# Diagonal tap blocks of a depthwise convolution, written ahead of time and read back as weight panels

## The chip, the cores and the metric

The kernel runs on one core of one Trainium2 chip. The metric is device time in microseconds (us) from start to end of one execution. Several engines run their own instruction streams beside each other: TensorE (PE, matmuls; PEld is its weight load), VectorE (DVE), ScalarE (ACT), GpSimd (POOL) and SyncE (SP), whose queue issues most DMAs. They meet only at semaphores.

## The reference

The program is a four-layer encoder over 512 tokens with 1024 features: retention, convolution, gated linear attention, retention, each followed by a squared-ReLU MLP. The two parts that the change touches:

```python
def rotary(t, positions):              # q and k of every retention head
    inv_freq = ROPE_BASE ** (-jnp.arange(half, dtype=F32) / half)
    ang = positions.astype(F32)[:, None, :, None] * inv_freq
    cos, sin = jnp.cos(ang), jnp.sin(ang)
    return jnp.concatenate([t1 * cos - t2 * sin, t2 * cos + t1 * sin], axis=-1)

def conformer_conv(u, w_in, b_in, w_dw, b_dw, ln_gain, ln_bias, w_out, b_out):
    a, gate = jnp.split(u @ w_in + b_in, 2, axis=-1)
    h = a * jax.nn.sigmoid(gate)
    h = lax.conv_general_dilated(h, w_dw[:, None, :], (1,), [(15, 15)],
        feature_group_count=D_MODEL) + b_dw      # 31 taps, each feature by itself
    h = jax.nn.silu(layernorm(h, ln_gain, ln_bias))
    return h @ w_out + b_out
```

The layer norm runs over the 1024 features of a token, so it needs the finished convolution of all features.

## The kernel before

Features lie on the 128 partitions and tokens along the free axis, so a tensor is eight tiles of 128x512. Every fp32 product is made of three matmuls of split operands (`mm3`, L433 to L442: high by high, low by high, high by low; the profile's L439, L440, L441). A weight panel is 128x1024: SyncE's queue loads it (512 KB), ScalarE rounds the high part, `whi` (L146), and VectorE subtracts it to get the low part, `wlo` (L147). A ring of six such pairs feeds TensorE; `Stream` (L100 to L235) fills it ahead of use. Some panels are split once, stored to DRAM in two parts and later loaded ready (`cut`).

TensorE's instructions run in the order of the code. The code also names work that is put off: `after(us, fn)` runs `fn` in the program when the matmuls written since then add up to that many us, and `flush` runs what is left. The order on ScalarE, VectorE and GpSimd is chosen by a scheduler when the program is built, except for the engines named in a `manual_schedule` block, where the code's order stands.

**The first retention** (L779 to L985). Its angles are positions times frequencies in turns, and they need more than fp32's digits: `angles` (L728 to L777) splits them into a high and a low part (`ahi`, `alo`), and GpSimd makes 24 operations of 128x512 for five larger pieces of the frequency (L757 to L764), summed up in `acc`. VectorE takes off whole turns (`wrap`, L747 to L749), adds the smaller pieces (L770) and makes a sine and a cosine (`sr`, `cr`), which also go to DRAM for the last retention. For each head, `rotated` multiplies the projected q and k by them (L850 to L852) and splits them into `qkh` and `qkl`. For head 0, TensorE does the values, q and k, then four gate projections (scaled by VectorE at L868, `o`), then the scores of q and k (`scores`, L915), which need `qkh` and `qkl`.

**The convolution** (L988 to L1187). Two projections make each feature tile (`hc`). The 31 taps of a tile are shared among the engines by the table `taps` in `run` (L1530): a pair says how many taps TensorE has, and how many ScalarE and GpSimd have together; VectorE has the rest.

- On TensorE a tap is a diagonal 128x128 matrix of that tap's weights, times the shifted tokens. ScalarE makes the high block `dh` (L1047), GpSimd the low blocks `dl`, four at a time, by an `affine_select` (L1043), while the convolution runs.
- On the side, ScalarE multiplies (L1056) and GpSimd adds (L1058, `side_taps`).
- On VectorE a tap is a multiply-add onto the sum in PSUM (L1073, `vec_taps`).

Then `center` takes a mean off and adds each tile to sums over all tiles (L1088, L252, L254). The statistics are matmuls with ones (L260); from them come the mean and the variance (L1140), and each tile is centered, scaled, put through SiLU and split into `zh` and `zl` (L1147 to L1154), the input of the output projection. All of this is done by halves of 256 tokens.

Of the kernel before, what the change touches and what calls it, by code (L numbers as in the profile page):

```python
# [21 lines left out]
P = 128  # L22
T = 512
# [71 lines left out]
class Stream:  # L95


    def __init__(self, K, src, ahead):
        self.K, self.src, self.ahead = K, src, ahead
        self.n = src.shape[0]  # L100
        self.ready, self.loaded, self.at = [], 0, 0
        self.deep = 5
        self.aside = {}
        self.cut = {}
        self.pairs, self.steps = {}, []

# [4 lines left out]
    def prep(self, parts=1):  # L111
# [8 lines left out]
        i = self.loaded  # L120
        if i in self.pairs:
            self.pair(i)
            return []
        self.loaded += 1
        if i in self.cut:
            hi, lo = self.aside.pop(i, self.ring)()
            pan = Panel(hi, lo)
            self.ready.append(pan)
            for tiles, src in zip((hi, lo), self.cut[i]):
                for t, x in enumerate(tiles):  # L130
                    nc.sync.dma_start(x.bitcast(F32), src[:, t * pan.w:(t + 1) * pan.w])
            return []
# [195 lines left out]
class Kern:  # L328
# [658 lines left out]

    def conv(self, layer, close):  # L988
        nc = self.nc
        with self.tc.tile_pool(name="conv", bufs=1) as op:  # L990
            self.W.keep(3 * KD - 4, [_spare(op, "w", 8)] * 4)
            with self.tc.tile_pool(name="taps", bufs=1) as cp:
                hc, sg = {}, {}
                co = [None] * KD
                msum = Sums(self, D)
                ident = cp.tile([P, P], F32, name="ident")
                nc.gpsimd.memset(ident, 1.0)
                nc.gpsimd.affine_select(ident, ident, pattern=[[-1, P]], compare_op=ALU.is_equal, fill=0.0, base=0, channel_multiplier=1)
# [17 lines left out]
                whi = cp.tile([P, KD * CW], F32R, name="wdh")  # L1016
                wlo = cp.tile([P, KD * CW], F32, name="wdl")
                wall = self.cst[:, _COLS["conv_w_dw"]:_COLS["conv_w_dw"] + KD * CW]
                nc.vector.tensor_copy(whi, wall)
                nc.vector.tensor_tensor(wlo, wall, whi.bitcast(F32), ALU.subtract)  # L1020
                shift = cp.tile([P, T], F32, name="shift")
                vsum = Sums(self, D)

                parts, sums = {}, {}

# [8 lines left out]
                def diag_taps(i):  # L1034

                    npe, _ = self.taps[i]
                    xh, xl = parts[i]
                    sums[i] = self.ps()
                    for t0 in range(0, npe, 4):
                        n = min(4, npe - t0)  # L1040
                        j = i * CW + t0
# [18 lines left out]
                def vec_taps(tiles, pieces=FULL):  # L1060

                    for t in range(CW):
                        for i in tiles:
# [5 lines left out]
                            if npe == 0 and t == nsw:  # L1069
# [4 lines left out]
                    for i in tiles:  # L1074
                        for lo, hi in pieces:
                            a, b = co[i][:, lo:hi], shift[:, lo:hi]
                            nc.vector.scalar_tensor_tensor(a, sums[i][:, lo:hi], self.col("conv_b_dw", i), a if self.taps[i][1] else b, ALU.add, ALU.add if self.taps[i][1] else ALU.subtract)

                def center(tiles, c=(0, T)):
                    for i in tiles:  # L1080
                        a = co[i][:, c[0]:c[1]]

                        if i == 0:
                            st = self.st()
                            nc.tensor.matmul(st, lhsT=self.ones[D], rhs=a, start=True, stop=True)
                            nc.scalar.activation(shift, st, AF.Copy, scale=float(KD))
                        if self.taps[i][1]:
                            nc.vector.tensor_tensor(a, a, shift[:, c[0]:c[1]], ALU.subtract)  # L1088
                        vsum.add(a, c)
                        msum.add(a, c, square=False)  # L1090
# [5 lines left out]

                self.lead(4, inp, us=4.0)
                pair(2)
                pair(3)
                side_taps(0)  # L1100
                side_taps(1)
                cut_taps(2)
                vec_taps((0, 1))
                self.after(self.shift_at, lambda: center((0, 1)))
# [583 lines left out]
```

## Time and profile before

| | us |
|---|---|
| median of 3 runs | 2718.35 (2717.16 to 2718.38) |
| the profiled execution's own time | 2716.43 |
| its span, first to last instruction | 2714.7 |
| TensorE busy | 2655.4 (98%) |
| VectorE busy | 1937.0 (71%) |
| ScalarE busy | 1363.1 (50%) |
| GpSimd busy | 135.2 (5%) |

The profile is of one execution. Busy times of the engines overlap each other. A wait of TensorE is given with the instruction that ended it. PEclk is the granted TensorE clock as a share of full speed.

### The profile page before, as it was taken

How to read it: one execution, taken by the hardware profiler on the slowest of the kernel's cores; microseconds unless marked ns; L12 is line 12 of the kernel's file. 1: busy time of each engine (PE TensorE's matmuls, PEld its weight loads, DVE VectorE, ACT ScalarE, POOL GpSimd, SP SyncE). 2: the span in 40 equal slices, each digit the busy share in tenths (PEclk: the TensorE clock that was granted, in tenths of full speed). 3: DMA queues.
4: the chain of work that ended last, by engine and by line, in shares of the span. 5: the costliest groups of instructions: out<-in, count | busy, mean ns of one | idle time of the engine just before them, and what ended most of it. 6: DMA issues, size and time to landing. Idle time of an engine off the chain costs nothing.

```text
span 2714.7 us, 38029 instructions
## 1 busy us (share of the span) xinstructions
PE 2655.4 (98%) x15040; PEld 2332.1 (86%) x15040; DVE 1937.0 (71%) x3045; ACT 1363.1 (50%) x2153; POOL 135.2 (5%) x133
## 2 busy tenths in 40 slices
PE   9999999999999699999999999999999999999998
PEld 7788889889998498999987888899888888989997
DVE  7755568878859977766788686777765565777766
ACT  5442445655537555544476555455544443555432
POOL 4000000000009500000000000000000000000000
PEclk9999999999999899999999999999999999999999
DMA  5223232686644012332222232333213222223322
GB/s 176 79 72 101 70 101 78 246 277 231 222 187 158 16 47 86 109 117 71 86 71 78 74 112 64 109 109 114 89 63 93 86 70 86 86 86 109 117 63 70
DMA packets 82692, 290.28 MB, mean 107 GB/s; under 512 B 9168, under 2 KB 11472, under 8 KB 82512
## 3 DMA queue, kind: packets, MB, share of 16 engines
q1 hardware_dynamic: 82368, 287.77, 32.5%
q8 instruction: 118, 1.93, 0.3%
q14 instruction: 62, 0.51, 0.1%
q10 hardware_dynamic: 144, 0.07, 0.0%
HBM read 260.02 MB, written 27.79 MB: 106 GB/s over the span
## 4 chain that ended last, share of the span: by engine, by line
PE 83%; DVE 8%; ACT 3%; DMA 2%; POOL 2%; issue 1%; SPq 0%; DVEq 0%; POOLq 0%; ACTq 0%
PE ps L440 27%; PE ps L441 27%; PE ps L439 27%; POOL y L1058 2%; DVE wlo L147 1%; DVE ps L1073 1%; DMA wraw<-in_wst_dram 1%; DVE acc L252 1%; DMA cuth<-whi 1%; DMA cutl<-wlo 1%; DVE tmp L314 1%; ACT whi L146 0%; DVE actl L427 0%; DVE h L317 0%; PE st L260 0%
## 5 line engine op out<-in xcount | busy, mean ns | idle before, releaser
L439 PE MATMUL ps<-xh,whi 128*128 128x256 f32 (+1 forms) x1792 | 600.3, 335 | 0.9 <-ACT xh L422 0.9
L440 PE MATMUL ps<-xl,whi 128*128 128x256 f32 (+1 forms) x1792 | 597.7, 334 | 1.1 <-DVE xl L429 1.1
L441 PE MATMUL ps<-xh,wlo 128*128 128x256 f32 (+1 forms) x1792 | 597.3, 333 | 0.0
L146 ACT ACTIVATE whi<-wraw 128x1024 fp32r<-128x1024 f32 (+1 forms) x300 | 312.2, 1045 | 315.5 <-PE ps L440 212.8
L147 DVE TENSOR_TENSOR wlo<-wraw,whi 128x1024 fp32r<-128x1024 f32 (+1 forms) x300 | 365.6, 1222 | 109.3 <-ACT whi L146 108.0
L440 PEld LDWEIGHTS ps<-xl,whi 128*128 128x128 f32 x1792 | 340.2, 190 | 35.9 <-DVE xl L429 1.5
L439 PEld LDWEIGHTS ps<-xh,whi 128*128 128x128 f32 x1792 | 340.3, 190 | 35.3 <-ACT xh L422 1.1
L441 PEld LDWEIGHTS ps<-xh,wlo 128*128 128x128 f32 x1792 | 340.2, 190 | 33.5
L440 PE MATMUL ps<-actl,whi 128*128 128x512 f32 x896 | 350.1, 391 | 3.6 <-DVE actl L427 3.5
L439 PE MATMUL ps<-acth,whi 128*128 128x512 f32 x896 | 349.0, 389 | 0.1
L441 PE MATMUL ps<-acth,wlo 128*128 128x512 f32 x896 | 348.7, 389 | 0.0
L293 DVE TENSOR_TENSOR y<-y,ps 128x512 f32<-128x512 f32 (+1 forms) x200 | 114.7, 579 | 210.3 <-PE ps L441 209.7
L439 PE MATMUL ps<-wS,whi 128*128 128x256 f32 x768 | 217.5, 283 | 1.3 <-ACT tmp L639 1.3
L440 PE MATMUL ps<-wS,whi 128*128 128x256 f32 x768 | 217.3, 283 | 0.0
L441 PE MATMUL ps<-wS,wlo 128*128 128x256 f32 x768 | 217.3, 283 | 0.0
L440 PEld LDWEIGHTS ps<-actl,whi 128*128 128x128 f32 x896 | 168.2, 188 | 42.6 <-DVE actl L427 8.9
L439 PEld LDWEIGHTS ps<-acth,whi 128*128 128x128 f32 x896 | 168.2, 188 | 35.6 <-ACT acth L420 0.8
L441 PEld LDWEIGHTS ps<-acth,wlo 128*128 128x128 f32 x896 | 168.2, 188 | 34.6
L175 ACT ACTIVATE whi<-wraw 128x1024 fp32r<-128x1024 f32 x96 | 101.5, 1057 | 144.5 <-PE ps L440 111.2
L175 ACT ACTIVATE whi<-raw 128x1024 fp32r<-128x1024 f32 x96 | 81.2, 846 | 160.0 <-PE ps L440 128.2
L252 DVE TENSOR_TENSOR acc<-acc,sq 128x256 f32<-128x256 f32 (+1 forms) x245 | 118.4, 486 | 51.2 <-ACT sq L251 45.4
L439 PEld LDWEIGHTS ps<-wS,whi 128*128 128x128 f32 x768 | 147.4, 192 | 1.7 <-ACT tmp L639 1.7
(350 smaller groups left out, 5348.8 us busy)
## 6 DMA issues: line engine op xcount, KB each, us to landing
wraw<-in_wst_dram SPq DMA_DIRECT2D x390, 512.0 KB, 3.6
raw<-in_wst_dram SPq DMA_DIRECT2D x48, 512.0 KB, 4.3
cuth<-whi SPq DMA_DIRECT2D x24, 512.0 KB, 3.8
cutl<-wlo SPq DMA_DIRECT2D x24, 512.0 KB, 3.8
whi<-cuth SPq DMA_DIRECT2D x20, 512.0 KB, 3.4
wlo<-cutl SPq DMA_DIRECT2D x20, 512.0 KB, 4.6
h<-in_xT_dram SPq DMA_DIRECT2D x8, 256.0 KB, 5.3
wraw<-in_wst_dram SPq DMA_DIRECT2D x8, 256.0 KB, 5.4
```

The lines of the kernel that those rows point to most:

```text
L146: nc.scalar.activation(h, raw[:, c:d], AF.Copy)
L147: nc.vector.tensor_tensor(l, raw[:, c:d], h.bitcast(F32), ALU.subtract)
L175: nc.scalar.activation(hi[0][:, :w], raw[:, :w], AF.Copy)
L252: nc.vector.tensor_tensor(acc, acc, t, ALU.add)
L293: self.K.nc.vector.tensor_tensor(y, y, ps[:, a:b], ALU.add)
L314: nc.vector.scalar_tensor_tensor(ts[k][:, a:b], self.ys[k][:, a:b], K.gain(self.layer, self.which, k), self.r[:, a:b], ALU.mult, ALU.mult)
L439: mm(out, lhsT=A[0], rhs=B[0], start=start, stop=False)
L440: mm(out, lhsT=A[0], rhs=B[1], start=False, stop=False)
L441: mm(out, lhsT=A[1], rhs=B[0], start=False, stop=stop)
L1058: nc.gpsimd.tensor_tensor(co[i], co[i], o, ALU.add)
L1073: nc.vector.scalar_tensor_tensor(sums[i], x, w, sums[i], ALU.mult, ALU.add)
```

## The change

Diagonal blocks, high and low, are made in `diagonals` by GpSimd in the first retention, 128x512 (four taps) at a time, each stored to DRAM by a DMA from GpSimd's own queue, through three buffers. There are eleven panels of eight taps. In the convolution they pass through the weight ring: `between` puts them among the convolution's own weight panels, and SyncE's queue loads them, two 512 KB parts each. The blocks `dh` and `dl`, and the identity, are gone from the convolution.

The table of taps is another one: TensorE 64 to 88 taps, ScalarE and GpSimd 68 to 73, VectorE 116 to 87. The taps of the last two tiles on TensorE run by halves of the tokens: both tiles for the first half (`c0`), then both for the second (`c1`). The statistics and the norm of the first half are put into the second half's taps (`after(5.0, first)`), those of the second half into the output projection (`after(4.5, second)`). The tiles Z are taken from the pool earlier, and four spare panels of the output projection later.

```diff
+        if self.between.get(i):
+            self.whole(self.between[i].pop(0), self.ring)
+            return []
...
+    def whole(self, parts, alloc):
+
+        hi, lo = alloc()
+        pan = Panel(hi, lo)
+        self.ready.append(pan)
+        for tiles, src in zip((hi, lo), parts):
+            for t, x in enumerate(tiles):
+                self.K.nc.sync.dma_start(x.bitcast(F32), src[:, t * pan.w:(t + 1) * pan.w])
+
+    def take(self, n, ahead):
+
+        self.fill(n + ahead)
+        out, self.ready = self.ready[:n], self.ready[n:]
+        return out
...
+            diags = self.diagonals(rp) if layer == 0 else None
...
+                    if diags:
+                        diags(h)
...
+    def diagonals(self, pool):
+
+        nc = self.nc
+        first = 2 * N_MLP
+        whi = pool.tile([P, KD * CW], F32R, name="wdh")
+        wlo = pool.tile([P, KD * CW], F32R, name="wdl")
+        wall = self.cst[:, _COLS["conv_w_dw"]:_COLS["conv_w_dw"] + KD * CW]
+        nc.vector.tensor_copy(whi, wall)
+        nc.vector.tensor_tensor(wlo, wall, whi.bitcast(F32), ALU.subtract)
+        todo = []
+        for i in range(KD):
+            for t in range(0, self.taps[i][0], 8):
+                at = self.W.between.setdefault(first + min(2 * i + 6, 2 * KD), [])
+                parts = [self.tc.dram_tile([P, 8 * P], F32, name=f"diag{n}{i}_{t}") for n in "hl"]
+                at.append(parts)
+                todo.append((i * CW + t, parts))
+        share = -(-len(todo) // (HEADS - 1))
+
+        def make(h):
+            for j, parts in todo[(h - 1) * share:h * share]:
+                for w, dst in zip((whi, wlo), parts):
+                    for a in (0, 4):
+                        d = pool.tile([P, 4 * P], F32R, name="dg", tag="dg", bufs=3)
+                        nc.gpsimd.affine_select(d.rearrange("p (t c) -> p t c", c=P), w[:, j + a:j + a + 4].bitcast(F32).unsqueeze(2).to_broadcast([P, 4, P]), pattern=[[0, 4], [-1, P]], compare_op=ALU.is_equal, fill=0.0, base=0, channel_multiplier=1)
+                        nc.gpsimd.dma_start(dst[:, a * P:(a + 4) * P], d.bitcast(F32))
+
+        return make
...
-            self.W.keep(3 * KD - 4, [_spare(op, "w", 8)] * 4)
+            Z = [self.pair(op, "z", 2 * KD) for _ in range(KD)]
...
-                        dl = cp.tile([P, 4 * P], F32R, name="dl", tag="dl", bufs=2)
-                        nc.gpsimd.affine_select(dl[:, :n * P].rearrange("p (t c) -> p t c", c=P), wlo[:, j:j + n].unsqueeze(2).to_broadcast([P, n, P]), pattern=[[0, n], [-1, P]], compare_op=ALU.is_equal, fill=0.0, base=0, channel_multiplier=1)
-                        for t in range(t0, t0 + n):
-                            dh = cp.tile([P, P], F32R, name="dh", tag="dh", bufs=4)
-                            j = i * CW + t
-                            nc.scalar.activation(dh, ident, AF.Identity, scale=whi[:, j:j + 1].bitcast(F32))
-                            self.mm3(sums[i], (dh, dl[:, (t - t0) * P:(t - t0 + 1) * P]), (xh[:, t:t + T], xl[:, t:t + T]), t == 0, t == npe - 1)
+                def diag_taps(i, pan, out, c=(0, T)):
+
+                    n = self.taps[i][0]
+                    for t in range(n):
+                        self.mm3(out, pan[t // 8].blk(t % 8), self.cut(parts[i], (t + c[0], t + c[1])), t == 0, t == n - 1)
...
+                    pan = self.W.take(self.taps[j][0] // 8, 3)
+                    sums[j] = self.ps()
+                    diag_taps(j, pan, sums[j])
...
-                vec_taps((KD - 2,))
-                with self.tc.manual_schedule(engines={ACT}):
...
+                n6, n7 = (self.taps[i][0] // 8 for i in (L6, L7))
+                pan = self.W.take(n6 + n7, 1)
+                H = T // 2
+                last = {}
+
+                def taps(c):
+                    last[c] = self.ps()
+                    diag_taps(L6, pan[:n6], last[c][:, :H], c)
+                    diag_taps(L7, pan[n6:], last[c][:, H:], c)
...
+                def complete(c):
+                    a, b = c
+                    y = co[L6][:, a:b]
+                    nc.vector.scalar_tensor_tensor(y, last[c][:, :H], self.col("conv_b_dw", L6), y, ALU.add, ALU.add)
+                    y = co[L7][:, a:b]
+                    nc.vector.tensor_tensor(y, last[c][:, H:], y, ALU.add)
+                    count(L6, c)
+                    count(L7, c)
...
+                def stats(c):
+                    a, b = c
+                    mu[c] = msum.mean(c, self.ps())
+                    sq = vsum.mean(c, self.ps())
+                    nc.scalar.activation(var[:, a:b], mu[c][:, a:b], AF.Square)
...
+                with self.tc.manual_schedule(engines={ACT, DVE}):
+                    less_shift(L6)
+                    less_shift(L7)
+                    taps(c0)
+
+                    def first():
+                        complete(c0)
+                        stats(c0)
+                        norm(c0)
+                        finish(c0, 0, 1, 2, 3)
+
+                    self.after(5.0, first)
+                    taps(c1)
+                    self.flush()
+                    complete(c1)
+                    finish(c0, 4, 5, 6)
...
+                    def second():
+                        stats(c1)
+                        finish(c0, 7)
+                        norm(c1)
+                        finish(c1, *range(KD))
+
+                    self.after(4.5, second)
+                    pan = self.W.group(4)
+                    pss = [self.ps() for _ in range(4)]
...
+            with self.tc.tile_pool(name="outw", bufs=1) as wp:
...
+                self.W.keep(0, [_spare(wp, "w", 8)] * 4)
...
-        self.taps = [(0, 10)] * 2 + [(6, 10)] * 2 + [(7, 10)] * 2 + [(10, 8), (28, 0)]
-        self.shift_at = 60.0
+        self.taps = [(0, 12), (8, 12), (8, 10), (8, 10), (8, 10), (16, 8), (24, 7), (16, 4)]
+        self.shift_at = 40.0
```

GpSimd at the start of the program. Before, the angles stand alone (`k`, `f` and `acc` are the angles' work tiles, `ahi` their input):

```order
L795 CAST dist<-disti 128x896
L757 TENSOR_SCALAR k<-ahi 128x512
L759 TENSOR_SCALAR f<-ahi 128x512
L758 TENSOR_SCALAR k<-k 128x512
L764 TENSOR_TENSOR acc<-f,k 128x512
```

After, the blocks (`dg`, from the high and low tap weights `wdh` and `wdl`) and their stores to DRAM (`diagh`, `diagl`) stand among them:

```order
L1028 AFFINE_SELECT dg<-wdh 128x512 x2
L1029 DMA diagh_0_215<-dg 128x512 x2
L1028 AFFINE_SELECT dg<-wdl 128x512 x2
L771 TENSOR_SCALAR k<-ahi 128x512
L773 TENSOR_SCALAR f<-ahi 128x512
L1029 DMA diagl_0_216<-dg 128x512 x2
L772 TENSOR_SCALAR k<-k 128x512
L1028 AFFINE_SELECT dg<-wdh 128x512 x2
L778 TENSOR_TENSOR acc<-f,k 128x512
L1029 DMA diagh_0_217<-dg 128x512 x2
L1028 AFFINE_SELECT dg<-wdl 128x512
```

It goes on like this: ahead of the angles' last addition stand 22 of the 44 selects and 21 of the 44 stores, four and two of them ahead of the first angle operation.

VectorE in head 0 of the first retention. Before, the wrap of the angles (`k`, `acc`) comes right after the split of the last values (`vl`), and the splits of further weight panels (`wlo`) and the gates (`o`) come in and behind it:

```order
L429 SCALAR_TENSOR_TENSOR vl_441<-ps_214,rcol_209,vh_440 128x512
L747 TENSOR_SCALAR k_454<-acc_453 128x512
L748 TENSOR_SCALAR k_454<-k_454 128x512
L147 TENSOR_TENSOR wlo_632<-wraw_630,whi_631 128x1024
L749 TENSOR_TENSOR acc_453<-acc_453,k_454 128x512
L770 SCALAR_TENSOR_TENSOR acc_453<-ahi_449,acc_453 128x512 x2
L770 SCALAR_TENSOR_TENSOR acc_453<-alo_450,acc_453 128x512 x2
L747 TENSOR_SCALAR k_454<-acc_453 128x512
```

After, four panel splits and three gates moved ahead of the wrap, and the fourth gate stands right behind its first three operations:

```order
L882 TENSOR_TENSOR o_721<-ps_696,rx_406 128x512
L146 TENSOR_TENSOR wlo_913<-wraw_911,whi_912 128x1024
L882 TENSOR_TENSOR o_755<-ps_730,rx_406 128x512
L146 TENSOR_TENSOR wlo_1069<-wraw_1067,whi_1068 128x1024
L761 TENSOR_SCALAR k_480<-acc_479 128x512
L762 TENSOR_SCALAR k_480<-k_480 128x512
L763 TENSOR_TENSOR acc_479<-acc_479,k_480 128x512
L882 TENSOR_TENSOR o_789<-ps_764,rx_406 128x512
L784 SCALAR_TENSOR_TENSOR acc_479<-ahi_475,acc_479 128x512
L146 TENSOR_TENSOR wlo_1075<-wraw_1073,whi_1074 128x1024
```

From the wrap's first operation to the last split of k's low part there were six panel splits and three gates; now there are one and one, `wlo_1075` and `o_789`.

VectorE at the end of the convolution. Before, the sums of all tiles (`acc`) come first, whole or by halves, then the variance of both halves (L1140), then the tiles (`y`):

```order
L252 TENSOR_TENSOR acc_7160<-acc_7160,sq_8635 128x512
L254 TENSOR_TENSOR acc_7151<-acc_7151,y_8617 128x256 x2
L252 TENSOR_TENSOR acc_7160<-acc_7160,sq_8645 128x256 x2
L1140 TENSOR_TENSOR tmp_8674<-ps_8677,tmp_8674 128x256
L1140 TENSOR_TENSOR tmp_8674<-ps_8681,tmp_8674 128x256
L1147 TENSOR_TENSOR y_7623<-y_7623,ps_8675 128x256
L1147 TENSOR_TENSOR y_7652<-y_7652,ps_8675 128x256
L452 SCALAR_TENSOR_TENSOR tmp_8695<-tmp_8674,eps_89,tmp_8683 128x256
L453 SCALAR_TENSOR_TENSOR tmp_8695<-tmp_8695,tmp_8683 128x256
```

After, the second half's sums, and the tiles 4 to 6 of the first half (scaled at L1194, centered at L1174, split at L441), stand ahead of the second half's variance (L1182). These are the last rows ahead of it:

```order
L1194 TENSOR_TENSOR y_8336<-y_8336,ro_8603 128x256
L1174 TENSOR_TENSOR y_8543<-y_8543,ps_8799 128x256
L1194 TENSOR_TENSOR y_8494<-y_8494,ro_8603 128x256
L1174 TENSOR_TENSOR y_8563<-y_8563,ps_8799 128x256
L441 TENSOR_TENSOR zl_7315<-y_8336,zh_7314 128x256
L1194 TENSOR_TENSOR y_8543<-y_8543,ro_8603 128x256
L441 TENSOR_TENSOR zl_7317<-y_8494,zh_7316 128x256
L441 TENSOR_TENSOR zl_7319<-y_8543,zh_7318 128x256
L1182 TENSOR_TENSOR tmp_8604<-ps_8989,tmp_8604 128x256
L1194 TENSOR_TENSOR y_8563<-y_8563,ro_8603 128x256
L441 TENSOR_TENSOR zl_7321<-y_8563,zh_7320 128x256
L1174 TENSOR_TENSOR y_7722<-y_7722,ps_8987 128x256
```

From the last panel split, `wlo_9242`, to that variance there are sixteen operations of 128x256.

## Rows read from the trace of the kernel before

**Rows 1.** The page's first part: busy us, share of span, instructions.
```profile
PE 2655.4 (98%) x15040; PEld 2332.1 (86%) x15040; DVE 1937.0 (71%) x3045; ACT 1363.1 (50%) x2153; POOL 135.2 (5%) x133
```

**Rows 2.** TensorE's waits: who waits, for whom, us in total, times, longest.
```profile
PE ps L260 <- DVE acc L254: 16.4, 1, 16.4
PE ps L439 <- ACT zh L420: 4.2, 1, 4.2
```

**Rows 3.** Stretches: busy us by engine, granted clock (PEclk), DMA share, GB/s.
```profile
core 0: us, PE busy (x) PEld busy (x) DVE busy (x) ACT busy (x) POOL busy (x), PEclk, DMA share, GB/s
808.00:836.00 28.00, 28.00 (x124) 22.82 (x123) 25.72 (x37) 18.88 (x28) 18.28 (x13) 1.00 0.74 289
...
922.00:941.00 19.00, 2.59 (x10) 1.83 (x9) 18.99 (x33) 3.90 (x6) 0.00 (x0) 0.63 0.00 0
948.00:952.00 4.00, 3.70 (x16) 3.53 (x17) 3.75 (x12) 3.03 (x7) 0.00 (x0) 0.50 0.02 6
```

**Rows 4.** TensorE's timeline in the convolution: start, duration, instruction, idle before.
```profile
803.52 0.40 PE L439 MATMUL ps<-xh,whi 128*128 128x512 f32 x1
...
940.44 3.70 PE L260 MATMUL ps<-acc,ones 128*128 128x256 f32 x8 [16.41 <-DVE acc L254]
948.30 0.58 PE L439 MATMUL ps<-zh,whi 128*128 128x256 f32 x1 [4.16 <-ACT zh L420]
...
954.34 0.28 PE L439 MATMUL ps<-zh,whi 128*128 128x256 f32 x1
...
974.13 0.28 PE L439 MATMUL ps<-zh,ww 128*128 128x256 f32 x1
```

**Rows 5.** The convolution's groups, busy us and mean ns, and GpSimd's selects.
```profile
L1073 DVE SCALAR_TENSOR_TENSOR ps<-hc,cst,ps 128x512 f32<-128x512 f32 x114 | 78.3, 743 | 0.0
L1058 POOL TENSOR_TENSOR y<-y,pr 128x512 f32<-128x512 f32 x61 | 86.0, 1419 | 34.7 <-ACT pr L1056 32.4
...
L1043 POOL TENSOR_SCALAR_AFFINE_SELECT dl<-wdl x18: 401/634/1093, 783.3 to 918.6; 128x512 fp32r<-128x512 f32 x13, 128x256 fp32r<-128x256 f32 x3, 128x384 fp32r<-128x384 f32 x2
```

**Rows 6.** GpSimd's timeline, the angles: the first, fifteenth and last of 24.
```profile
20.79 3.22 POOL L757 TENSOR_SCALAR k<-ahi 128x512 f32<-128x512 f32 x1 [18.04 <-ACT ahi L742]
...
42.62 0.62 POOL L757 TENSOR_SCALAR k<-alo 128x512 f32<-128x512 f32 x1
...
50.59 1.30 POOL L762 TENSOR_TENSOR acc<-acc,f 128x512 f32<-128x512 f32 x1
```

**Rows 7.** VectorE's timeline from the wrap to the last split of k.
```profile
51.92 0.43 DVE L747 TENSOR_SCALAR k<-acc 128x512 f32<-128x512 f32 x1 [6.98 <-POOL acc L762]
...
54.59 1.42 DVE L770 SCALAR_TENSOR_TENSOR acc<-ahi,acc 128x512 f32<-128x512 f32 x2
...
79.15 1.22 DVE L147 TENSOR_TENSOR wlo<-wraw,whi 128x1024 fp32r<-128x1024 f32 x1
80.29 0.68 DVE L427 TENSOR_TENSOR qkl<-tmp,qkh 128x512 fp32r<-128x512 f32 x1
80.89 0.69 DVE L868 TENSOR_TENSOR o<-ps,rx 128x512 f32<-128x512 f32 x1
```

**Rows 8.** TensorE's timeline at the end of the gates and the first scores.
```profile
71.19 0.39 PE L440 MATMUL ps<-xl,whi 128*128 128x512 f32 x1
...
77.54 0.39 PE L441 MATMUL ps<-xh,wlo 128*128 128x512 f32 x1
...
79.29 0.50 PE L441 MATMUL ps<-qkh,qkl 128*128 128x512 f32 x1 [0.91 <-DVE qkl L427]
```

**Rows 9.** The start: ScalarE's DMA issue, its split of the angles, a VectorE sum.
```profile
0.78 0.41 ACTq L346 DMA_DIRECT2D cst<-in_cst_dram  x1
...
20.09 0.61 ACT L742 ACTIVATE ahi<-ang 128x512 fp32r<-128x512 f32 x1
...
18.42 0.42 DVE L252 TENSOR_TENSOR acc<-acc,sq 128x256 f32<-128x256 f32 x1
```

**Rows 10.** DMA issues: out, in, queue, count, KB, us from issue to landing.
```profile
dram_sin<-sr SPq DMA_DIRECT2D x1, 256.0 KB, 2.6
dram_cos<-cr SPq DMA_DIRECT2D x1, 256.0 KB, 2.0
```

More of the change, by code (lines that the diff above doesn't have):

```diff
@@ L105, in __init__ @@
         self.pairs, self.steps = {}, []
+        self.between = {}
     def ring(self):
@@ L125, in prep @@
         if i in self.cut:
[L126 to L131, printed above, removed]
+            self.whole(self.cut[i], self.aside.pop(i, self.ring))
             return []
@@ L994, in conv @@
                 co = [None] * KD
[L995 to L998, printed above, removed]
+                msum, vsum = Sums(self, D), Sums(self, D)
+                shift = cp.tile([P, T], F32, name="shift")
+                parts, sums = {}, {}
                 def inp(n, ps, c):
@@ L1074, in vec_taps, with less_shift, count, center @@
                     for i in tiles:
[L1075 to L1079, printed above, removed]
+                        nc.vector.scalar_tensor_tensor(co[i], sums[i], self.col("conv_b_dw", i), co[i], ALU.add, ALU.add)
+                def less_shift(i):
+                    nc.vector.tensor_tensor(co[i], co[i], shift, ALU.subtract)
+                def count(i, c=(0, T)):
+                    a = co[i][:, c[0]:c[1]]
+                    vsum.add(a, c)
+                    msum.add(a, c, square=False)
+                def center(tiles):
                     for i in tiles:
-                        a = co[i][:, c[0]:c[1]]
                         if i == 0:
                             st = self.st()
-                            nc.tensor.matmul(st, lhsT=self.ones[D], rhs=a, start=True, stop=True)
+                            nc.tensor.matmul(st, lhsT=self.ones[D], rhs=co[0], start=True, stop=True)
                             nc.scalar.activation(shift, st, AF.Copy, scale=float(KD))
[L1087 to L1090, printed above, removed]
+                        less_shift(i)
+                        count(i)
                 def pair(i):
@@ L1095, in pair @@
                         self.when(lambda n=n, ps=ps: inp(n, ps, (0, T)))
+                L6, L7 = KD - 2, KD - 1
                 self.lead(4, inp, us=4.0)
                 pair(2)
[L1099 removed]
                 side_taps(0)
[L1101 to L1104, printed above, removed]
[L1105 to L1113 removed]
@@ L1127, in conv @@
[L1127 to L1149 removed]
+                cut_taps(1)
@@ new lines, in conv @@
+                vec_taps((0,))
+                for i in range(3, KD):
+                    pair(i)
+                    j = i - 2
+                    pan = self.W.take(self.taps[j][0] // 8, 3)
+                    sums[j] = self.ps()
+                    diag_taps(j, pan, sums[j])
+                    side_taps(j)
+                    cut_taps(j + 1)
+                    if j == 1:
+                        vec_taps((1,))
+                        self.after(self.shift_at, lambda: center((0, 1)))
+                    elif j % 2 == 1:
+                        vec_taps((j - 1, j))
+                        self.after(0.1, lambda j=j: center((j - 1, j)))
@@ L1150, in finish, with norm @@
+                def norm(c):
+                    less_mean(0, c)
+                    less_mean(1, c)
+                    self.rsqrt_newton(rs, var, seed, c)
+                def finish(c, *tiles):
+                    for i in tiles:
                         z = co[i][:, c[0]:c[1]]
@@ L1173, in outp @@
-                def outp(n, ps, c):
-                    lo, hi = c
-                    nc.vector.tensor_scalar(close.y(n)[:, lo:hi], ps[:, lo:hi], self.col("conv_b_out", n), None, ALU.add)
-                pan = self.W.group(4)
-                pss = [self.ps() for _ in range(4)]
-                for c in HALVES:
-                    for k in range(KD):
-                        for i in range(4):
-                            self.mm3(pss[i][:, c[0]:c[1]], pan[i].blk(k), self.cut(Z[k], c), k == 0, k == KD - 1)
+                        if i + 2 < KD:
+                            less_mean(i + 2, c)
```

96 lines of the change are left out of this document (25 added, 71 removed).

## The prediction, made before the changed kernel ran

> **What bounds the kernel now.** I read the page's totals first, then TensorE's waits, then the two stretches that the change touches. TensorE works 98% of the span [rows 1], so the time is its matmuls plus its waits, and an edit counts where it adds or removes matmuls or moves one of these waits. The longest, 16.4 us, is at the end of the convolution, where the statistics wait for VectorE's last sums; 4.2 us more follow at the first normalized tile [rows 2]. The stretch before shows why: in 19.00 us TensorE is busy 2.59 and VectorE 18.99 [rows 3]. So VectorE bounds the convolution's end. The granted clock is 0.50 in 948 to 952 [rows 3], the lower level (1.2 GHz), after TensorE had stood nearly idle for some 24 us.
>
> The other stretch is head 0 of the first retention. GpSimd works out the rotary angles from 20.79 to 51.89 us [rows 6]. VectorE waits 6.98 us for them and then wraps them, rotates q and k and splits them, until 80.97 [rows 7]. TensorE meets the results with a wait of 0.91 us [rows 8]. That chain has almost no slack: what delays the angles by more than a little delays TensorE.
>
> **The convolution's gain.** I take the stretch from the projection that starts at 803.52 to the end of the first output group, 974.13 [rows 4], and lay TensorE's new work on it without a wait, at full clock. A matmul of 512 columns comes every (77.54 - 71.19)/28 = 0.227 us [rows 8], one of 256 every (974.13 - 954.34)/165 = 0.120 us [rows 4].
> - 12 projections (two for each of tiles 2 to 7) of 24 matmuls: 65.3 us.
> - Tiles 1 to 5 have 8, 8, 8, 8 and 16 taps on TensorE, 48, each three matmuls: 32.7 us.
> - Tiles 6 and 7, 24 + 16 = 40 taps, by halves: 240 matmuls of 256 columns, 28.8 us.
> - Statistics: the eight matmuls take 3.70 us at half clock [rows 4], so 1.9; the shift and the rest as much again: 3.8.
> - The output group: 192 matmuls of 256 columns, 23.0 us.
> Together 153.6 us: it would end at 957.1, 17.0 earlier than now, if nothing waited.
>
> Does anything wait? VectorE has 116 - 87 = 29 fewer taps of 743 ns [rows 5], some 20 us, and would end about 920 for 940; the first half's taps end on TensorE at 803.52 + 65.3 + 32.7 + 14.4 + 1.9 = 917.8. That is close, but VectorE's last sums of that half are due only 5 us into the second half's taps. GpSimd gains 73 - 68 = 5 tap products less a first one per tile, 4 additions of 1419 ns, and loses 18 selects of 634 ns [rows 5]. A diagonal panel is 1 MB and feeds 24 matmuls, 5.4 us: 193 GB/s, where 808 to 836 moved 289 [rows 3]. So these I cost at nothing.
>
> What is late next is the chain from the statistics to the first normalized tile, 948.30 - 940.44 = 7.9 us [rows 4]. For the first half it lies beside 8.6 us of the second half's taps. For the second half, 6.5 us of output matmuls are left when its statistics are issued: a wait of at least 1.4 us. In VectorE's order (third pair of order rows) about sixteen operations of 128x256 still stand ahead of that chain, 0.42 us each [rows 9], 6.7 us: at most 8.1. I take 5, nearer the middle, because part of the sixteen run before the statistics are issued. The gain is 17.0 - 5 = 12.0 us, with bounds of 15.6 and 9.
>
> **The first retention's loss.** The diagonal blocks are 44 selects of 128x512, each followed by a DMA that GpSimd issues. The code writes them for heads 1 to 3, but in GpSimd's order (first pair of order rows) 22 selects and 21 issues stand before the last angle operation, 18 and 19 of them behind the first angle operation. VectorE's wrap waits for the last one, everything of head 0 is queued behind the wrap, and TensorE, once through gate 4's projection, has only the scores to do.
>
> The first angle operation starts at 21.4: its input is ready at 20.09 + 0.61 [rows 9], and VectorE's two casts ahead of it add some 0.7; the four selects before it fit ahead of that, since the second weight table comes after the sum at 18.42 [rows 9]. From there:
> - Angle operations: the first 14 took 42.62 - 20.79 = 21.83 us, beside a busy VectorE, 1.56 each, the last ten 51.89 - 42.62 = 9.27, 0.93 each [rows 6]. Stretched out by the selects, I put 9 in the busy time and 15 in the quiet one: 27.9 us.
> - Selects: 18 x 0.634 [rows 5] = 11.4 us.
> - Issues: 19 x d. The trace has no issue by GpSimd. The low bound is ScalarE's issue, 0.41 us [rows 9]. The high one is an issue that holds the engine until the data has landed, 2.0 us for 256 KB [rows 10]. I take d = 1.0, some two times from either end: 19 us.
> The angles end at 60.7 + 19 d = 79.7, for 51.89 now; at 68.5 with the low bound, at 98.7 with the high one.
>
> The Trainium skill, "DMA: Bandwidth & Descriptors", section Specifications, gives a DMA issued by GpSimd about 1 us to its first byte against some 0.6 for the hardware queues, and its section on the anatomy of a GpSimd DMA a fixed cost of about 2 us, mostly completion. If only the first held the engine, the sum, an estimate, would stay where it is; if the second did, it would go to the high end. No run shows either yet.
>
> From the start of the wrap to the last split of k VectorE takes 80.97 - 51.92 = 29.05 us [rows 7]. In it are six panel splits, 80.29 - 79.15 = 1.14 from start to start, and three gate operations, 0.60 like the operation at 80.29 [rows 7]: bare, it is 20.4. In the new order (second pair of order rows) only one split and one gate operation stand in it: 22.2. So q and k are ready at 101.9, 20.9 us later; TensorE already waited there, so all of it is delay. And there is a floor. Gate 4's operation stands behind the first wrap, and waits for TensorE, which starts the last matmul of gate 4 at 77.54 and ends it at 77.93 [rows 8]. However early the angles come, the chain behind its first three operations (54.59 - 51.92 - 1.14 = 1.53 us [rows 7]) cannot go on before that: q and k at 77.93 - 1.53 + 22.2 = 98.6, a delay of 17.6. The floor decides for d up to 0.83.
>
> Such a wait has a second price. After the convolution's idle stretch 27 matmuls took 954.34 - 948.30 = 6.04 us [rows 4], for 3.24 at full clock. I add the same 2.8 us here; it is 0 if the clock is kept.
>
> The other 22 selects and 23 issues stand behind the angles, where GpSimd has no work until the selects at 783.3 [rows 5], and the panels are read some 700 us later. I cost them at nothing.
>
> Sum: -12.0 + 20.9 + 2.8 = +11.7 us on the profiled execution's own 2716.43: 2728.1. The median of the runs, 2718.35, stands 1.9 above that execution, so the forecast is 2730.
>
> **Rivals.**
> 1. Cheap issues: d is at or under 0.83, the floor decides, and the output waits little. For it: 0.41 us where an issue is seen [rows 9]. Against: that is another engine's queue. +17.6 + 2.8 - 15.6 = +4.8: 2723.
> 2. An issue holds GpSimd until its data has landed. For it: there are three buffers for the blocks, so a select waits for the store three before it. Against: that leaves three stores in flight, and the angle operations stand between. Delay 98.7 + 22.2 - 81.0 = 39.9: +39.9 + 2.8 - 12 = +30.7, 2749.
> 3. The convolution keeps its wait: VectorE comes 10 us late, not 2, to the first half's sums, so that both halves' chains are open. For it: VectorE's end stands within 3 us of the taps' end. Against: 20 us of taps are gone. Gain 3: +20.7, 2739.
> 4. Faster: q and k ready in time because VectorE's chain is not bound by gate 4. It decides when the delay is under about 9 us, which needs the chain to start by 67.6: the angles done by then (d under 0.37) and gate 4's operation not behind the wrap. For it: GpSimd could issue beside its operations. Against: the order rows put gate 4 there. With a delay of 9, no lower clock and a gain of 15.6: -6.6, 2712.
>
> **How the numbers follow.** A measurement of this kernel can tell 0.2%, 5.4 us, from no change, so "the same" is 2712.9 to 2723.8. Chances: the forecast 0.57 (its own range 2724 to 2738), the first rival 0.16, the second 0.14, the third 0.07, the fourth 0.06. The first counts as the same, though half a us from its edge; the fourth as faster; the rest as slower. Faster 0.06, the same 0.16, slower 0.78. The range starts at 2717, where the floor meets the whole 17 us of gain and a kept clock (+0.6, less what the extra 1.9 is uncertain by), and ends at 2755, where the high bound of d meets the small gain: +39.9 + 2.8 - 9 = +33.7, 2752, and a little for the third rival on top.
>
> **What would show it.** Right: TensorE's longest wait is at head 0's first scores, about 21 us, ended by the split of q or k near 102; GpSimd's last angle addition ends near 80, with issues of about 1 us between the selects; the granted clock is at its lower level after the wait; the 16.4 us wait is gone, and one of some 5 us stands in the output group. Wrong: the wait at the scores is under 15 us or over 30, GpSimd's issues take half or twice the time, or the convolution's stretch is shorter by less than 9 us.

## The result and the profile after

The changed kernel takes 2766.7 us (median of 4 runs, 2763.19 to 2768.97) for 2718.07 of the kernel before on the same chip: 1.0178 times, 95% interval 1.0161 to 1.0196. The forecast said slower, 2730, with a range up to 2755: the sign was right, the size was not.

TensorE's waits after the change (engine, line and tile that waited, for whom; us in total, times, longest):

```profile
PE ps L453 <- ACT qkh L434: 46.5, 2, 46.0
...
PE ps L453 <- ACT zh L434: 3.4, 2, 1.9
PE ps L454 <- DVE xl L1065: 3.2, 1, 3.2
PE ps L453 <- ACT xh L1064: 2.9, 1, 2.9
```

The 16.4 us of [rows 2] are gone, and 46.0 us stand at the first scores of head 0. Two other waits are new, at the split operands `xh` and `xl` of the last tile's taps.

GpSimd's timeline shows the 46 us. The selects (L1028), stores (L1029) and angle operations (L771 to L778), with the idle time before each:

```profile
16.77 5.43 POOL L1028 TENSOR_SCALAR_AFFINE_SELECT dg<-wdh 128x512 fp32r<-128x512 f32 x2 [14.02 <-DVE wdh L1012]
22.15 0.79 POOL L1029 DMA_DIRECT2D diagh<-dg  x1
26.64 0.57 POOL L1029 DMA_DIRECT2D diagh<-dg  x1 [3.70 <-issue]
27.21 4.23 POOL L1028 TENSOR_SCALAR_AFFINE_SELECT dg<-wdl 128x512 fp32r<-128x512 f32 x2
31.53 0.93 POOL L771 TENSOR_SCALAR k<-ahi 128x512 f32<-128x512 f32 x1
...
96.19 1.26 POOL L776 TENSOR_TENSOR acc<-acc,f 128x512 f32<-128x512 f32 x1
...
112.41 0.59 POOL L1029 DMA_DIRECT2D diagl<-dg  x1 [0.90 <-POOL dg L1028]
115.06 0.54 POOL L1029 DMA_DIRECT2D diagl<-dg  x1 [2.07 <-issue]
115.61 1.23 POOL L1028 TENSOR_SCALAR_AFFINE_SELECT dg<-wdh 128x512 fp32r<-128x512 f32 x2
117.66 0.58 POOL L1029 DMA_DIRECT2D diagh<-dg  x1 [0.82 <-POOL dg L1028]
```

The angles end at 97.45, for 51.89 in [rows 6]. An issue shows 0.55 to 0.8 us itself, but the next follows 2.6 us after it (112.41, 115.06, 117.66), and the two selects between the last two cost nothing extra: what holds the next issue lets GpSimd compute. What that is, the half stores below tell. At the start the first four selects take 2.1 to 2.7 us each, for 0.6 later, and an issue 4.5 (22.15 to 26.64).

VectorE's wrap, its last split of k, and TensorE behind it:

```profile
97.48 1.14 DVE L761 TENSOR_SCALAR k<-acc 128x512 f32<-128x512 f32 x1 [25.07 <-POOL acc L776]
...
124.09 0.69 DVE L441 TENSOR_TENSOR qkl<-tmp,qkh 128x512 fp32r<-128x512 f32 x1 [0.69 <-ACT qkh L434]
```

```profile
121.71 0.79 PE L453 MATMUL ps<-qkh 128*128 128x512 f32 x1 [46.04 <-ACT qkh L434]
...
131.42 0.39 PE L453 MATMUL ps<-poh,vh 128*128 128x512 f32 x1
```

VectorE sits idle for 25.07 us in front of the wrap, until GpSimd's last addition. The last row, the first matmul of head 0's output, stood at 85.46 before: 45.96 us later. From there to the convolution 2.3 us more are lost, 0.7 in each of heads 1 to 3. The convolution's stretch of [rows 4]:

```profile
851.75 0.40 PE L453 MATMUL ps<-xh,whi 128*128 128x512 f32 x1
...
964.11 0.38 PE L453 MATMUL ps<-xh,whi 128*128 128x256 f32 x1 [2.93 <-ACT xh L1064]
967.73 0.58 PE L454 MATMUL ps<-xl,whi 128*128 128x256 f32 x1 [3.24 <-DVE xl L1065]
...
996.05 1.13 PE L274 MATMUL ps<-acc,ones 128*128 128x256 f32 x4 [0.25 <-DVE acc L268]
...
1019.75 0.28 PE L453 MATMUL ps<-zh,ww 128*128 128x256 f32 x1
```

It takes 168.0 us for 170.6: a gain of 2.6. So the span's 46.8 are 46.0 + 2.3 - 2.6, and 1.2 behind the convolution that I didn't follow up. The clock in four stretches (busy us by engine, granted clock, DMA share, GB/s), two at each place:

```profile
core 0: us, PE busy (x) PEld busy (x) DVE busy (x) ACT busy (x) POOL busy (x), PEclk, DMA share, GB/s
78.00:121.70 43.70, 0.00 (x0) 0.00 (x0) 22.41 (x31) 3.75 (x6) 25.71 (x40) 0.50 0.32 117
121.70:129.30 7.60, 7.12 (x15) 4.87 (x16) 4.46 (x7) 1.48 (x3) 3.32 (x6) 0.50 0.23 87
960.90:967.70 6.80, 0.66 (x4) 0.26 (x2) 6.80 (x10) 1.18 (x2) 3.00 (x3) 0.84 0.00 0
967.70:972.40 4.70, 4.67 (x22) 4.67 (x23) 4.70 (x8) 0.00 (x0) 0.00 (x0) 0.51 0.00 0
```

After both waits TensorE goes on at the lower level (1.2 GHz). VectorE is busy in the whole of the third and fourth stretch: it still bounds the convolution.

### The profile page after: what moved, and what is told of

The parts are those of the page before. It is cut to its first block, busy times and chain, and to the rows that moved or that the text cites. A ratio compares the mean times of both kernels' runs of the same rounds, so it can differ in the third digit from the quotient of the medians.

```text
span 2761.5 us, 38433 instructions
## 1 busy us (share of the span) xinstructions
PE 2673.8 (97%) x15232; PEld 2351.8 (85%) x15232; DVE 1931.5 (70%) x3022; ACT 1348.6 (49%) x2097; POOL 181.6 (7%) x205
## 4 chain that ended last, share of the span: by engine, by line
PE 80%; DVE 9%; POOL 3%; ACT 3%; DMA 3%; issue 2%; DVEq 0%; SPq 0%; ACTq 0%; POOLq 0%
PE ps L454 26%; PE ps L455 26%; PE ps L453 26%; POOL y L1082 1%; DMA wraw<-in_wst_dram 1%; DVE wlo L146 1%; DMA cuth<-whi 1%; POOL dg L1028 1%; DVE ps L1097 1%; ACT whi L145 1%; DVE acc L266 1%; DMA cutl<-wlo 0%; DVE tmp L328 0%; DVE h L331 0%; DVE actl L441 0%
## 5 line engine op out<-in xcount | busy, mean ns | idle before, releaser
L453 PE MATMUL ps<-xh,whi 128*128 128x256 f32 (+1 forms) x1920 | 643.4, 335 | 3.9 <-ACT xh L1064 2.9
L454 PE MATMUL ps<-xl,whi 128*128 128x256 f32 (+1 forms) x1920 | 640.3, 334 | 4.3 <-DVE xl L1065 3.2
L455 PE MATMUL ps<-xh,wlo 128*128 128x256 f32 (+1 forms) x1920 | 639.8, 333 | 0.0
L454 PEld LDWEIGHTS ps<-xl,whi 128*128 128x128 f32 x1920 | 365.4, 190 | 41.8 <-DVE xl L1065 3.4
L453 PEld LDWEIGHTS ps<-xh,whi 128*128 128x128 f32 x1920 | 365.4, 190 | 40.8 <-ACT xh L1064 3.1
L455 PEld LDWEIGHTS ps<-xh,wlo 128*128 128x128 f32 x1920 | 365.5, 190 | 36.0 <-DVE wlo L146 0.4
```

The costliest lines, as they stand in the source:

```text
L453: mm(out, lhsT=A[0], rhs=B[0], start=start, stop=False)
L454: mm(out, lhsT=A[0], rhs=B[1], start=False, stop=False)
L455: mm(out, lhsT=A[1], rhs=B[0], start=False, stop=stop)
```

## The experiments

Theory A: GpSimd's selects and stores in front of the angles are the loss. The rivals: VectorE's order, the stores' traffic, or the new convolution. A ratio is to the kernel before on the same chip as the run; its median there was 2717.91 us for the first four runs, 2716.74 for the three after head 0, with the pad and with the split early, 2716.94 for the rest. Times of different groups are best compared by their ratios.

**The angles first.** GpSimd's order as written, so that the blocks stand behind the angles:

```diff
+            if layer == 0:
+                with self.tc.manual_schedule(engines={POOL}):
+                    self.retention(layer, j, close)
```

> Changed kernel, with GpSimd's instructions of the first retention in the order in which the code is written, so that all selects and stores stand behind the angles. Theory A (the loss is the selects and stores in front of the angles): the angles end near 52 us as before the change, TensorE's wait at head 0's first scores falls from 46.0 to under 3 us, and the time is 2766.7 - 46 = 2721 (2716 to 2725). Rival B (the wait comes from VectorE's order, gate 4 behind the wrap, or from the stores' traffic): a wait of over 10 us stays, 2731 or more.

2726.03 us (7 runs, 1.0027 times before, 1.0015 to 1.0038). The angles end at 52.34, and the wait at the scores is 3.1 us in two pieces:

```profile
PE st L285 <- ACT sq L435: 3.7, 1, 3.7
...
PE ps L456 <- DVE qkl L442: 3.1, 2, 1.7
```

40.7 of the 48.6 us are back. Of B, the stores' traffic falls: all 44 stores are still made, from 53 us on. VectorE's order went back with GpSimd's, to six panel splits and three gates in its chain, so this run doesn't tell the two apart; the 25.07 us in which VectorE sat idle in front of the wrap do, and that part of B falls by them. The time is a us above the range given. The first norm's wait of 3.7 us (1.0 before) is part of the rest, and so is VectorE's chain, beside which the selects now run. Its last split of k, which ended at 80.97 before, with the angles done 0.45 us earlier:

```profile
84.87 1.22 DVE L442 TENSOR_TENSOR qkl<-tmp,qkh 128x512 fp32r<-128x512 f32 x1
```

**The blocks alone.** The kernel before, with `diagonals` of the change added and its panels read by nobody.

> Kernel before the change, with the diagonal blocks made and stored as in the change, but read by nothing: the convolution is the old one. Theory A: the loss is all there, angles end near 97 us, wait of 46 us, and the output projections of heads 1 to 3 run 0.7 us longer each: 2718 + 46 + 2 = 2766 (2761 to 2770). Rival D (the new convolution or its panels cost a good part): under 2755.

2770.24 us (1.0192, 1.0177 to 1.0208), a quarter of a us above A's range; the wait is there, and the old convolution's too:

```profile
PE ps L439 <- ACT qkh L420: 46.9, 2, 46.4
PE ps L260 <- DVE acc L254: 15.9, 1, 15.9
```

D falls: the new convolution is worth the 3.5 us between this and the change.

**The stores by SyncE.**

```diff
-                        nc.gpsimd.dma_start(dst[:, a * P:(a + 4) * P], d.bitcast(F32))
+                        nc.sync.dma_start(dst[:, a * P:(a + 4) * P], d.bitcast(F32))
```

> Changed kernel, scheduler's own order (selects among the angles), but the stores are issued by SyncE's queue. Theory A (the issues hold GpSimd, some 2 us each behind the 0.6 that show): without them the angles end at 55 to 65 us and TensorE's wait is under 15 us, 2720 to 2735. Rival C (the selects, slowed beside a busy VectorE, are the cost): the angles end after 80, 2745 or more.

2740.77 us (1.0082, 1.0067 to 1.0097). GpSimd's last angle operation, and TensorE's wait:

```profile
66.44 1.29 POOL L776 TENSOR_TENSOR acc<-acc,f 128x512 f32<-128x512 f32 x1
```

```profile
PE ps L453 <- ACT qkh L434: 16.5, 1, 16.5
```

The angles end at 67.73, between the two forecasts. Of the delay of 45.1 us (97.45 - 52.34) the 21 issues make 97.45 - 67.73 = 29.7, 1.4 each beside what they hide, and the selects, 23 in this run's order, 67.73 - 52.34 = 15.4, 0.7 each. Both theories have a part, the issues two thirds.

**Two forms of half a store.** The angles first, and each store in two:

```diff
+                            if w is whi:
+                                o = slice(2 * b * P, 2 * (b + 1) * P)
+                                nc.gpsimd.dma_start(dst[:, a * P:(a + 4) * P][:, o], d[:, o].bitcast(F32))
+                            else:
+                                o = slice(b * P // 2, (b + 1) * P // 2)
+                                nc.gpsimd.dma_start(dst[o, a * P:(a + 4) * P], d[o].bitcast(F32))
```

> As the run with the angles first, but each store is cut in two: those of the high parts by columns (128 rows of 1 KB), those of the low parts by rows (64 rows of 2 KB). Read from the trace: the time from one issue of GpSimd to the next where nothing waits, 2.65 us for a whole store in the changed kernel. Theory A1 (a fixed cost per issue): 2.65 us for both. A2 (a cost per row): 2.65 for the column halves, 1.3 to 1.6 for the row halves. A3 (a cost per byte, or the landing): 1.3 to 1.6 for both. The total, within 3 us of the run with the angles first under each.

GpSimd's timeline, `diagh` by columns, `diagl` by rows:

```profile
103.84 0.60 POOL L1033 DMA_DIRECT2D diagh<-dg  x1 [0.83 <-POOL dg L1029]
106.27 0.54 POOL L1033 DMA_DIRECT2D diagh<-dg  x1 [1.83 <-issue]
...
108.69 0.59 POOL L1033 DMA_DIRECT2D diagh<-dg  x1 [1.23 <-issue]
111.16 0.54 POOL L1033 DMA_DIRECT2D diagh<-dg  x1 [1.88 <-issue]
...
112.67 0.59 POOL L1036 DMA_DIRECT2D diagl<-dg  x1 [0.32 <-POOL dg L1029]
113.53 0.55 POOL L1036 DMA_DIRECT2D diagl<-dg  x1 [0.28 <-issue]
...
115.05 1.09 POOL L1036 DMA_DIRECT2D diagl<-dg  x2 [0.31 <-POOL dg L1029]
...
117.64 0.59 POOL L1033 DMA_DIRECT2D diagh<-dg  x1 [0.84 <-POOL dg L1029]
```

Column halves (128 rows) follow each other by 2.43, 2.42 and 2.47 us with half the bytes; four row halves (64 rows) take 117.64 - 112.67 = 4.97, 1.24 each. So a fixed cost per issue, A1, falls, and the numbers are near A2's forecast. But a time per row it is not: the changed kernel's whole stores, of 128 rows too, kept the next one off for 2.6 to 5.1 us ahead of the angles' end. Two of its issues on GpSimd's timeline:

```profile
38.64 0.55 POOL L1029 DMA_DIRECT2D diagl<-dg  x1 [4.08 <-issue]
...
43.72 0.60 POOL L1029 DMA_DIRECT2D diagh<-dg  x1 [1.40 <-issue]
```

What goes with the gap is the landing of the store before. The last number of a row is the time from issue to landing, in us, here of the changed kernel's stores issued at 22.15, 38.64 and 115.06:

```profile
diagh<-dg POOLq DMA_DIRECT2D x1, 256.0 KB, 4.2
...
diagl<-dg POOLq DMA_DIRECT2D x1, 256.0 KB, 4.8
...
diagl<-dg POOLq DMA_DIRECT2D x1, 256.0 KB, 2.3
```

The next issue came 4.49, 5.08 and 2.60 us after these, 0.3 after each landing. Of the 43 issues that follow another in the changed kernel none comes sooner than 0.3 us after the landing of the one before, and 39 come just then; the other four stand behind other work of GpSimd. So the next store waits for the landing. The halves in the timeline above, the columns first:

```profile
diagh<-dg POOLq DMA_DIRECT2D x5, 128.0 KB, 2.1
diagl<-dg POOLq DMA_DIRECT2D x4, 128.0 KB, 2.3
```

A column half behind a column half waits for the landing too, 2.1 us and 0.3. Row halves don't: up to three are under way at once, and in this run there were never more than 192 rows under way, in the changed kernel never more than 128. That fits a limit on rows under way, which no run tests by itself. A3 was right about the landing and wrong that half the bytes land in half the time.

The Trainium skill, "DMA: Bandwidth & Descriptors", section on the anatomy of a GpSimd DMA, has about 2.0 us plus bytes/436 GB/s: an estimate from it is 2.6 us for a whole store and 2.3 for either half. The trace agrees within 0.3 us where the landing was quickest (2.3, and 2.1 and 2.3 for the halves).

The whole took 2722.04 us in its one run, 4 us under the run with the angles first where 3 were allowed, but inside that run's own 2721.68 to 2728.84.

**The blocks after head 0.** The tables by GpSimd, behind a read of head 0's output:

```diff
+            if h == 1:
+                nc.gpsimd.tensor_copy(late, og[0][0][:, :1].bitcast(F32))
+                nc.gpsimd.tensor_copy(whi, wall)
+                nc.gpsimd.tensor_tensor(wlo, wall, whi.bitcast(F32), ALU.subtract)
```

> As the run with the angles first, but GpSimd also makes the two weight tables, waits for head 0's output before them, and so starts its selects only in head 1. Theory A: what was left of the loss, 4 us at the first norm (VectorE's two casts push its work into the angles' time) and up to 4 us in head 0's chain (selects beside VectorE), goes: 2726 - 4 to - 8, 2718 to 2722; the wait of the first norm's statistics falls from 3.7 to 1 us. Rival E (these are scatter of single runs, the rest is the convolution's): 2724 or more. The tiles of the first retention lie 4 bytes further than in that run.

2718.17 us (11 runs; 1.0001, 0.9992 to 1.0010): the whole loss is back, as A said, and E falls. The last split of k ends at 80.61, for 86.09 with the angles first. The first norm's wait was 2.5 us in the trace, not the 1 forecast, and 5.2 with the pad below, so it varies without the tables on VectorE too. The tables' engine and the selects' place were changed together, so their shares aren't told apart.

**Aligned by a pad.**

```diff
+        self.pad(pool, 15)
```

> As the run before it in this list, with a pad of 60 bytes per partition, so that the tiles behind the weight tables lie 2048 bytes further than before the change, not 1988. Theory F (the output projections' matmuls of heads 1 to 3 run 0.233 us apart for 0.227 because their operand tiles were shifted by a number of bytes that is no multiple of 128 or more): back to 0.227, 2.1 us less. Rival G (it is the traffic of the blocks' stores): no change in the pace.

2719.16 us (1.0005, 0.9996 to 1.0014), no gain: theory F, a matter of alignment to 128 bytes or more, falls. G forecast the unchanged pace, but its cause falls as well: head 3 loses its 0.7 us too, with its output projection 86 us behind the landing of the last store (353.4 for 267.8; in the changed kernel 395.5 for 161.4). The output projections of heads 1 to 3 here (busy us, mean ns):

```profile
L454 PE MATMUL ps<-poh,whi 128*128 128x512 f32 x96 | 37.9, 395 | 0.0
```

**Tables taken late**, from the pool behind the other tiles, and the angles in the old order (`k`, `f`, `k`), on top of the blocks after head 0 without the pad:

```diff
-        whi = pool.tile([P, KD * CW], F32R, name="wdh")
-        wlo = pool.tile([P, KD * CW], F32R, name="wdl")
+            if h == 1:
+                tables.extend(pool.tile([P, KD * CW], F32R, name=n) for n in ("wdh", "wdl"))
```

> As the run whose blocks start after head 0, with the two weight tables taken from the pool only then, behind the other tiles, and with GpSimd's angle operations in the order that the scheduler had given them before the change. Theory J (the place of the operand tiles in memory sets the pace of those output projections): 0.227 us between matmuls for 0.233, and the first norm as early as before: 2718 - 2 - 1 to 2 = 2714 to 2716, some 3 us below the kernel before, which is what the convolution's gain of 2.6 leaves. Rival K (the pace has another cause): 0.233 stays, 2716 to 2718.

2715.56 us (0.9995, 0.9986 to 1.0004). The same projections:

```profile
L454 PE MATMUL ps<-poh,whi 128*128 128x512 f32 x96 | 37.3, 389 | 0.0
```

Theory J: the tiles' place sets the pace. The angles' order, changed with it, does not: the changed kernel has the same order, and 394 ns there. The stores are still made, so G falls by this run too. From the first output matmul of head 0 to the convolution it takes 716.8 us, for 719.8 without this edit; 1.9 of the 3.0 are the pace, 22.17 us from the first to the last of the 96 matmuls of a head for 21.53. The gain in the whole time is within the scatter of the runs.

**The convolution: split early**, on top of the pad.

```diff
+                cut_taps(L7)
                 side_taps(L6)
                 side_taps(L7)
-                cut_taps(L7)
```

with `bufs=3` for `xh` and `xl`.

> As the run with the pad, and the split of tile 7 for its taps on TensorE gets a third pair of buffers and stands earlier in the code, so that it is done before tile 6's taps end. Theory H (the convolution's gain of 12 us shrank to 2.6 by the two waits of 2.9 and 3.2 us at tile 7's first taps and the lower clock behind them, 2 us): the waits go, 6 to 8 us less. Rival I (VectorE is still the bound, and the time goes to the wait at the statistics): under 3 us less, and a new wait of TensorE at the statistics matmuls.

2720.35 us (1.0014, 1.0005 to 1.0023). The waits at tile 7 are gone, and the statistics wait:

```profile
PE ps L275 <- DVE acc L269: 8.6, 2, 8.4
```

The stretch takes 172.0 us for 168.0 with the pad alone. Theory H falls for this kernel, I holds: VectorE is the bound.

**One more panel**, on top of the tables taken late.

```diff
-(8, 10), (16, 8), (24, 7), (16, 4)]
+(8, 10), (24, 7), (24, 7), (16, 4)]
```

> As the run before it in this list, with tile 5 at 24 taps on TensorE and 7 on the side, none on VectorE (80 vector taps for 87, 12 panels for 11). Theory L (VectorE bounds the convolution, TensorE has some 12 us of slack before the statistics): 7 taps of 0.66 us, 4 to 5 us less, TensorE's waits at tile 7's first taps fall below 3 us together. Rival M (TensorE or the panels' loads bound it by now): no change or up to 5.4 us more, the time of 24 more matmuls.

2718.75 us (1.0005, 0.9996 to 1.0014), stretch 173.1 for 169.1: 4 us longer, near the 5.4 of the 24 matmuls. L's forecast fails, and M's comes true in its number. The wait at tile 7 stays, since the split stands where it stood:

```profile
PE ps L455 <- DVE xl L1070: 4.6, 1, 4.6
```

**Both**, the panel and the split early, on top of the tables taken late.

> As the run with one more panel, and tile 7's split early with a third pair of buffers. Theory L: VectorE still ends last, so the wait stands at the statistics instead of at tile 7, within 2 us of that run. Rival H (the waits at tile 7 and the lower clock behind them are a cost of their own): 3 us less or more.

2712.14 us (11 runs; 0.9980, 0.9972 to 0.9989): faster than both kernels. The stretch is 164.8 us, and neither wait is left; this is the longest in it:

```profile
PE ps L454 <- ACT zh L435: 3.4, 2, 1.9
```

L's forecast for this run, no more than 2 us, was wrong: 6.6 us less than with the panel alone, as H said. M falls as a cause: the same matmuls and panels took 8.3 us less in the stretch. The split early alone moves the wait to the statistics, the panel alone leaves it at tile 7 with 24 matmuls more, and each clears what the other one leaves. The split early was run alone with the pad, not with the tables taken late.

## Why the prediction was wrong

**The step that failed: the end of the angles**, "60.7 + 19 d = 79.7". They ended at 97.45. The mechanism was right (the order rows gave it, and the angles first and the blocks alone show it); two terms of the sum were too small.
- "The first angle operation starts at 21.4 ... the four selects before it fit ahead of that": it started at 31.53, 10.1 late. I took 0.634 us for a select from [rows 5]; beside the busy VectorE at the start they took 2.1 to 2.7, 9.7 for the four. The two issues between them, which the sum leaves out there, took 5.1 more (22.15 to 27.21). The doubled angle operations of [rows 6] had shown that stretch for what it is. The Trainium skill, "SBUF — State Buffer", section "Who interferes with whom", says that a VectorE instruction with two inputs in that memory contends with a GpSimd instruction that reads it, and the trace agrees (5.43 us for two selects, 1.23 later).
- "I take d = 1.0": an issue keeps the next one off until its data has landed, 2.6 to 5.1 us. With what is hidden under it, it cost 1.4 (the stores by SyncE). From 31.53 the rest took 65.9 us for 58.3 in the sum.

The second rival, an issue that holds GpSimd until its data has landed, came nearest, 98.7 for the angles and 2749 for the time. Its mechanism was half right: the next issue waits for the landing, but GpSimd's operations between two issues go on. That 98.7 is so near is luck: 2.0 per issue for the 1.4 paid made up for the late start.

**The chain to q and k**: 22.2 us in the sum, 124.78 - 97.48 = 27.3 measured. The number of operations was right. Five pieces of it stood beside GpSimd's selects and took 4.3 us longer (the first wrap operation 1.14 us for 0.43 in [rows 7]); the rest are waits.

**The clock's price**: 2.8 in the sum. From the first score to the first output matmul it took 9.7 us for 7.7, so 2.0: right in kind, 0.8 too much.

**The floor of gate 4** did not decide, since the angles came later still.

**The convolution's gain**: 12.0 in the sum, 2.6 measured. Two steps failed. "VectorE would end about 920": it came to the first half's sums only at 977.68 on a clock 48.2 us later, 929.5. Its stretch in the two kernels (the kernel before first, columns as in the clock's table above):

```profile
803.52:940.30 136.78, 114.95 (x486) 91.36 (x484) 128.81 (x180) 84.67 (x157) 97.17 (x81) 0.94 0.31 116
...
851.75:977.68 125.93, 119.76 (x577) 100.67 (x576) 114.62 (x145) 65.65 (x98) 92.02 (x69) 0.97 0.51 184
```

29 taps less gave 11 us and not 20: VectorE was busy 14.2 us less (128.81 to 114.62), with 16.6 less in its taps (78.3 to 61.7) and 2.4 more in its other operations (the mean of `y<-y,shift` rose from 996 to 1271 ns), and it waited 3.3 us more. "These I cost at nothing": TensorE did not wait for the sums, as I had checked, but for the split of tile 7, the high part by ScalarE and the low part by VectorE, 6.2 us and some 2 at the lower clock. In VectorE's order that split stands behind its own taps and the sums of earlier tiles, ahead of the first half's sums:

```profile
966.97 0.71 DVE L1065 TENSOR_TENSOR xl<-hc,xh 128x542 fp32r<-128x542 f32 x1
...
977.68 0.48 DVE L1162 SCALAR_TENSOR_TENSOR y<-ps,cst,y 128x256 f32<-128x256 f32 x1
```

The wait in the output group, 5 in the sum, is 3.4. My count of TensorE's own work came out some 3 us short (168.0 less 153.6, less 9.8 of waits and 2 of clock).

**Not in the sum**: 0.7 us in each of heads 1 to 3, from the place of the tables in memory; I had costed what moves in time and nothing that moves in memory.

**The other 22 selects and 23 issues**, "at nothing" in the sum: not so in the changed kernel, where the selects right behind the angles go with the 4.3 us lost in the chain above. With all 44 behind the angles q and k came at 86.09 for 80.97 (the angles first). Only behind head 0 do they hide (80.61, the blocks after head 0).

## What to carry to other kernels

A scheduler may put work that is "for later" first (22 of the 44 selects here): read the order, and tie such work to something late by a data dependence. Price an operation from a row of the stretch in which it will run, not from a quiet one, and find the first consumer behind the engine that bounds a stage, not only the sum that it ends with. Where two waits stand in series on one bounded engine, edits against them have to be tried together.

## What the runs showed that I had not expected

A store issued by GpSimd keeps GpSimd's next store off until it has landed, while GpSimd's own operations go on: the next issue came 0.3 us after the landing, 2.6 to 5.1 us after the issue for the same 256 KB ahead of the angles' end. Stores of 64 rows did not wait like that: up to three were under way. And matmuls of the same shape come 3% slower (one in 0.233 us for 0.227, their mean time 395 ns for 389) with their operand tiles some 2 KB further in memory: a shift of 1984, 1988 or 2048 bytes did it, and taking it away undid it; what it is about the place stays open.
